# Halved block loads, regrouped stores and a load held back for the first store, in a DoRA projection on one core

## The chip, the cores and the metric

The kernel runs on one core of one Trainium2 chip. The metric is the device time of one execution in microseconds (us), as the median of several runs; lower is better. A core has five engines with an instruction stream each: TensorE (PE, its weight loads shown apart as PEld), VectorE (DVE), ScalarE (ACT), GpSimd (POOL) and SyncE (SP). They meet through semaphores. Transfers between HBM and the on-chip memory (SBUF) are issued by SP and by ACT here, each with a DMA queue of its own (q1 for SP, q10 for ACT), and are carried out by 16 DMA engines that serve both queues.

## What is computed

The reference, cut to what matters (x is 16 x 2048 x 256, W is 256 x 256, the LoRA rank is 16, all float32):

```python
W_adapted = W + scale * (lora_A @ lora_B)
W_norm = np.sqrt(np.sum(W_adapted ** 2, axis=0, keepdims=True) + 1e-8)
W_final = W_adapted / W_norm * m
y = x.reshape(-1, 256) @ W_final
```

So there is a small prologue that makes a 256 x 256 weight, and then one product over 32768 rows. x is 33.6 MB that are read, y is 33.6 MB that are written.

## The kernel before

**Tiling.** The rows are cut into 8 blocks of 4096 rows (4 MB each); a block is 8 chunks of 512 rows (512 KB), 64 chunks in all. Two chunks make a pair; there are 32 pairs. A block lies in one of five SBUF buffers (`x_bufs`, 128 partitions x 32 rows x 1 KB), so block 5 can be loaded only when block 0 has been stored from the same buffer. The product is written back over the x it came from. Inside a block each partition holds 32 consecutive rows, so a whole block is moved in pieces of 32 KB for each partition, half a block in pieces of 16 KB, and one chunk in pieces of 4 KB that lie 32 KB apart in HBM.

**One pair's way.** POOL rounds a pair to bf16 (L197, `xb`). TensorE transposes it in 8 steps into PSUM (`turned`, L302). DVE copies that to SBUF (L238, `xt`). TensorE multiplies, 8 matmuls for each of the two chunks (`product`, L316). ACT copies each chunk's product from PSUM over the chunk in `x_bufs` (L256). On TensorE the order is: turned(pair 0), and then a loop in which turned(p+1) stands ahead of product(p). TensorE takes one from the semaphores `rounded`, `copied` and `room` by hand (`take`).

**Prologue.** TensorE makes A^T and A·B (L272, L276), the column sums of squares (`n2_ps`, L283) and m spread over the partitions (`mb_ps`, L288), in that order. DVE makes `wa`, its square, `m_all` (L225), `wam` (L228), the reciprocal (L231) and `w_final` (L234); ACT makes the square root (L248). POOL's first rounding waits for DVE's fourth result (L192). Ahead of its loop TensorE waits until `w_final` is there (`dv` 8) and opens `room`; in that wait stands everything behind turned(0), turned(1) included.

**Loads (SP, in order).** W; then chunks 0-1, 2-3, 4-7; then blocks 1, 2 and 3 whole; then five chunks of block 4 and its last three chunks one by one (pieces of 4 KB). All these are issued at once, by 6 us. Then SP waits (L167) for stores 0, 1 and 2 and issues blocks 5, 6 and half of 7; the last half waits for store 3.

**Stores (ACT, in order).** Each stands behind ACT's copy of a chunk and a drain (L262). Block 0 behind chunk 21, block 1 behind chunk 22, block 2 in two halves behind chunk 24 (stores 0 to 3). Then chunks 24, 25, 26 and 27 one by one in pieces of 4 KB behind chunk 27; the rest of block 3 and blocks 4 and 5 behind chunk 47; block 6 behind chunk 55; block 7 in two halves behind chunks 59 and 63.

**Rest.** POOL holds pair 15 back until store 2 has landed (`REST`). At the very end SP waits for the later stores (L341).

Of the kernel before, what the change touches and what calls it, by code (L numbers as in the profile page):

```python
# [11 lines left out]
def kernel(  # L12
# [10 lines left out]
    nc = tc.nc  # L23
# [6 lines left out]
    x_flat = x.flatten_outer_dims()  # L30
    out_flat = out.flatten_outer_dims()
# [4 lines left out]
    J = 4  # L36
    DJ = 32
    BLK = DJ * P
    NBLK = N // BLK
# [3 lines left out]
    XBUFS = 5  # L43
    CH = DJ // J
    NCH = NBLK * CH

    NPR = NCH // 2
# [1 line left out]
    NXB = 2  # L49

    REST = 15
    IDLE = 8
    NXT = 2
    F8 = 2 * J * P

# [7 lines left out]
    def sb(name, shape, dtype):  # L63
        return ctx.enter_context(nc.sbuf_tensor(name, shape, dtype))
# [4 lines left out]
    x_bufs = [sb(f"x_sb{k}", [P, DJ, IN], FP32) for k in range(XBUFS)]  # L69
    xb_bufs = [sb(f"xb{k}", [P, 2 * J, IN], BF16) for k in range(NXB)]  # L70
# [4 lines left out]
    m_row = sb("m_row", [1, OUT], FP32)  # L75
    identity = sb("identity", [P, P], FP32)
    zeros = sb("zeros", [P, P], FP32)
    ones = sb("ones", [P, P], FP32)
# [18 lines left out]
    mb_ps = y_ps[1][:, 2, :]  # L97
# [3 lines left out]

    units = [(b * CH, CH) for b in range(NBLK - 1)]
    units += [(NCH - CH, CH // 2), (NCH - CH // 2, CH // 2)]
    loads = [(0, 2), (2, 2), (4, CH - 4)] + units[1 : XBUFS - 1]


    loads += [((XBUFS - 1) * CH, CH - 3)]
    loads += [(XBUFS * CH - 3 + c, 1) for c in range(3)] + units[XBUFS:]
    load_of = {g: n for n, (g0, cnt) in enumerate(loads) for g in range(g0, g0 + cnt)}

    F = NBLK - XBUFS
    G = F * CH
    stores = [(b * CH, CH, 21 + b) for b in range(F - 1)]
    stores += [(G - CH, CH // 2, 24), (G - CH // 2, CH // 2, 24)]
    FIRST = len(stores)
    stores += [(G + c, 1, G + 3) for c in range(4)]
    stores += [(G + 4, CH - 4, 47)]  # L120
    stores += [(b * CH, CH, max(47, (b + 1) * CH - 1)) for b in range(F + 1, NBLK - 1)]
    stores += [(g0, cnt, g0 + cnt - 1) for g0, cnt in units[-2:]]
    HALF = FIRST - 2


    late = [nc.alloc_semaphore(f"store{n}") for n in range(FIRST, len(stores))]
    sems = {f"store{FIRST + k}": s for k, s in enumerate(late)}

    def sem(name):
        if name not in sems:  # L130
            sems[name] = tc.alloc_semaphore(name)
        return sems[name]

    def in_sbuf(g0, cnt):
        b, c = divmod(g0, CH)
        return x_bufs[b % XBUFS][:, c * J : (c + cnt) * J, :]

    def in_dram(dram, g0, cnt):
        (u0, ucnt), = [u for u in units if u[0] <= g0 < u[0] + u[1]]
        unit = dram[u0 * J * P : (u0 + ucnt) * J * P].rearrange("(p j) k -> p j k", p=P)  # L140
        return unit[:, (g0 - u0) * J : (g0 - u0 + cnt) * J, :]

    def load_x(n):
        nc.sync.dma_start(
            out=in_sbuf(*loads[n]), in_=in_dram(x_flat, *loads[n])
        ).then_inc(sem(f"load{n}"), 16)

    def store_y(n):
        nc.scalar.dma_start(
            out=in_dram(out_flat, *stores[n][:2]), in_=in_sbuf(*stores[n][:2])  # L150
        ).then_inc(sem(f"store{n}"), 16)


    nc.sync.dma_start(
        out=w_nat[:], in_=W.rearrange("(p t) o -> p t o", t=KC)
    ).then_inc(sem("load_w"), 16)
    nc.scalar.dma_start(
        out=a_nat[:], in_=lora_A.rearrange("(p t) r -> p t r", t=KC)
# [1 line left out]
    nc.scalar.dma_start(out=b_nat[:], in_=lora_B).then_inc(sem("load_b"), 16)  # L160
    nc.scalar.dma_start(out=m_row[:], in_=m[None, :]).then_inc(sem("load_m"), 16)
    for n in range(len(loads)):
        if loads[n][0] == XBUFS * CH:


            for k in range(HALF + 1):
                nc.sync.wait_ge(sem(f"store{k}"), 16)  # L167
        if loads[n] == units[-1]:
            nc.sync.wait_ge(sem(f"store{HALF + 1}"), 16)
        load_x(n)  # L170


# [3 lines left out]
        out=identity[:],  # L176
        in_=zeros[:],
# [3 lines left out]
        pattern=[[-1, P]],  # L181
        channel_multiplier=1,
    ).then_inc(sem("ident"), 1)
    for p in range(NPR):
        b, c = divmod(p, PRB)
        for g in (2 * p, 2 * p + 1):
            if g == 0 or load_of[g - 1] != load_of[g]:
                nc.gpsimd.wait_ge(sem(f"load{load_of[g]}"), 16)
        if p == 0:


            nc.gpsimd.wait_ge(sem("dve"), 4)  # L192
        if p == REST:
            nc.gpsimd.wait_ge(sem(f"store{HALF}"), 16)
        if p >= NXB:
            nc.gpsimd.wait_ge(sem("turned"), p - NXB + 1)
        nc.gpsimd.tensor_copy(  # L197
            out=xb_bufs[p % NXB][:],
            in_=x_bufs[b % XBUFS][:, 2 * c * J : 2 * (c + 1) * J, :],
        ).then_inc(sem("rounded"), 1)  # L200

    nc.gpsimd.wait_ge(sem("turned"), NPR - NXB + 1)
    nc.gpsimd.memset(xb_bufs[NPR % NXB][:], 0.0).then_inc(sem("rounded"), 1)  # L203


    for _ in range(IDLE):
        nc.gpsimd.wait_ge(sem("ident"), 1)


    dv = sem("dve")  # L210
    nc.vector.memset(ones[:], 1.0)
# [8 lines left out]
        out=wa[:], in0=ab_ps, scalar=float(scale), in1=w_nat[:], op0=ALU.mult, op1=ALU.add  # L220
    ).then_inc(dv, 1)
    nc.vector.wait_ge(dv, 3)
    nc.vector.tensor_mul(out=sq[:], in0=wa[:], in1=wa[:]).then_inc(dv, 1)  # L223
    nc.vector.wait_ge(sem("pe"), 4)
    nc.vector.tensor_copy(out=m_all[:], in_=mb_ps).then_inc(dv, 1)  # L225
    nc.vector.wait_ge(dv, 5)
    for t in range(KC):
# [5 lines left out]
    for t in range(KC):  # L233
        i = nc.vector.tensor_mul(out=w_final[:, t], in0=wam[:, t], in1=rnorm[:])  # L234
    i.then_inc(dv, 1)
    for p in range(NPR):
        nc.vector.wait_ge(sem("turned"), p + 1)
        nc.vector.tensor_copy(  # L238
            out=xt_bufs[p % NXT][:].rearrange("p r t -> p (r t)").bitcast(FP32),
            in_=xt_ps[p % 2][:],  # L240
        ).then_inc(sem("copied"), 1)


    nc.scalar.wait_ge(dv, 1)

    nc.scalar.activation(out=warm[:], in_=eps_col[:], func=AF.Sqrt)  # L246
    nc.scalar.wait_ge(sem("pe"), 3)
    nc.scalar.activation(  # L248
        out=norm[:], in_=n2_ps, func=AF.Sqrt, bias=eps_col[:]
    ).then_inc(sem("act"), 1)  # L250
    drains = 0
    for g in range(NCH):
        b, c = divmod(g, CH)
        nc.scalar.wait_ge(sem("product"), g + 1)

        nc.scalar.copy(  # L256
            out=x_bufs[b % XBUFS][:, c * J : (c + 1) * J, :], in_=y_ps[g % 2][:]
        ).then_inc(sem("room"), 1)
        due = [n for n in range(len(stores)) if stores[n][2] == g]
        if due:  # L260
            drains += 1
            nc.scalar.drain().then_inc(sem("done"), 1)  # L262
            nc.scalar.wait_ge(sem("done"), drains)
            for n in due:
                store_y(n)


    pe = sem("pe")
# [6 lines left out]
    for t in range(KC):  # L275
        i = nc.tensor.matmul(  # L276
            ab_ps[:, t, :], aT[:, t * P : (t + 1) * P], b_bf[:], start=True, stop=True
        )
    i.then_inc(pe, 1)
    nc.tensor.wait_ge(dv, 4)  # L280

    for t in range(KC):
# [1 line left out]
            n2_ps, ones[:], sq[:, t, :], start=(t == 0), stop=(t == KC - 1)  # L284
        )
    i.then_inc(pe, 1)
    nc.tensor.wait_ge(sem("load_m"), 16)
    nc.tensor.matmul(mb_ps, ones[0:1, :], m_row[:], start=True, stop=True).then_inc(pe, 1)  # L288
    def take(name):

        nc.tensor.sem_inc(sem(name), -1).wait_op(sem(name), 1, "sem-ge")  # L291
# [4 lines left out]
        j_order.append(a + J // 2)  # L296

    def turned(p):
        take("rounded")

        for j in range(2 * J):
            i = nc.tensor.transpose(  # L302
                xt_ps[p % 2][:, j * P : (j + 1) * P],
                xb_bufs[p % NXB][:, j, :].bitcast(FP32),
                identity[:],
            )
        i.then_inc(sem("turned"), 1)

    def product(p):
        take("copied")  # L310
        for h in range(2):
            take("room")
            for t in range(KC):
                for j in j_order:
                    r = (h * J + j) * P
                    i = nc.tensor.matmul(  # L316
                        y_ps[h][:, j, :],
                        xt_bufs[p % NXT][:, r : r + P, t],
                        w_final[:, t, :],
                        start=(t == 0 and (j % (J // 2)) == 0),  # L320
                        stop=(t == KC - 1 and (j % (J // 2)) == (J // 2) - 1),
                    )
            i.then_inc(sem("product"), 1)

    turned(0)

    nc.tensor.wait_ge(dv, 8)
    nc.tensor.sem_inc(sem("room"), 2)
    with nc.Fori(0, NPR // 2, 1, engines=[PE], head_slot={PE: 128}):
        turned(1)  # L330
        product(0)
        turned(0)
        product(1)

# [1 line left out]
    critical.close()  # L336
    tc.close()
    tc.compile()
    for s in late:
        nc.sync.wait_ge(s, 16)  # L340
        nc.sync.sem_clear(s)  # L341


# [33 lines left out]
```

## Time and profile before

| what | value |
|---|---|
| median of 4 runs | 162.58 us (162.35 to 162.65) |
| the profiled execution's own time | 162.84 us |
| its span, first to last instruction | 161.5 us |
| moved by DMA | 67.42 MB, 417 GB/s over the span |
| busy: PE / PEld / DVE / ACT / POOL | 60% / 52% / 28% / 40% / 39% |
| TensorE idle in the middle (pair 15 held back) | 25 us, about 55 to 80 us |
| last product stored by ACT | issued at 132.25 us |

The profile's page has the span in 40 slices of 4.04 us with each engine's busy share, the DMA engines' busy share and the bytes that they moved; the chain of work that ended last; groups of instructions with their mean duration; and the DMA issues with the time from issue to landing. Besides the page, the timeline lists instructions in order of time, and the trace holds one record for each DMA packet (queue, start, duration, size) and the time of each semaphore update, a DMA's 16 completions among them. An engine that is idle costs something only where the last work of all waits for it.

### The profile page before, as it was taken

What the parts mean: (1) busy time and instruction counts of PE and PEld (TensorE: products, weight loads), DVE (VectorE), ACT (ScalarE), POOL (GpSimd) and SP (SyncE); (2) the same over time, 40 slices, a digit from 0 to 9 for tenths busy, and PEclk for the clock granted to TensorE, in tenths of its full rate; (3) what the DMA queues carried; (4) which work ended last, traced back from release to release, by engine and by line L of the source; (5) the groups of instructions that cost most, each with busy time, mean ns of one, the idle gap of its engine ahead of it and who ended that gap; (6) DMA issues with size and microseconds to landing.
All of it is one profiled execution on the core that took longest, in us unless ns stands there. A gap on an engine that the chain in (4) does not pass through costs nothing. (4 is left out here: it accounts for less than half of the span.)

```text
span 161.5 us, 2012 instructions
## 1 busy us (share of the span) xinstructions
PE 96.7 (60%) x786; PEld 84.8 (52%) x786; DVE 44.9 (28%) x44; ACT 64.0 (40%) x67; POOL 62.7 (39%) x39
## 2 busy tenths in 40 slices
PE   0493999999999600000199999999999940000000
PEld 0253798999998400000179999978899930000000
DVE  0447344354444300000033635353535300000000
ACT  3010366767767700000026686856786850000000
POOL 1264419677672000000674479197677100000000
PEclk9999999999999965555559999999999995555555
DMA  4999999999899999999999999999999999999895
GB/s 152 428 467 454 389 511 398 389 487 422 373 413 385 430 451 416 430 402 434 430 455 420 406 448 429 430 422 430 434 458 454 398 446 456 389 446 462 373 434 239
DMA packets 4356, 67.42 MB, mean 417 GB/s; under 512 B 625, under 2 KB 642, under 8 KB 1666
## 3 DMA queue, kind: packets, MB, share of 16 engines
q1 hardware_dynamic: 2160, 33.82, 49.4%
q10 hardware_dynamic: 2194, 33.59, 48.6%
q14 instruction: 2, 0.02, 0.0%
HBM read 33.85 MB, written 33.55 MB: 417 GB/s over the span
## 5 line engine op out<-in xcount | busy, mean ns | idle before, releaser
L256 ACT COPY x_sb<-y_ps 128x1024 f32<-128x1024 f32 x64 | 62.1, 1015 | 60.5 <-PE y_ps L316 59.9
L197 POOL CAST xb<-x_sb 128x2048 bf16<-128x2048 f32 x32 | 60.2, 1896 | 61.5 <-DMA out_dram<-x_sb 28.6
L316 PE MATMUL y_ps<-w_final,xt 128*128 128x256 bf16 x512 | 64.8, 282 | 0.8 <-PEq L291 0.7
L238 DVE COPY xt<-xt_ps 128x1024 f32<-128x1024 f32 x32 | 39.2, 1225 | 74.9 <-PE xt_ps L302 74.9
L316 PEld LDWEIGHTS y_ps<-w_final,xt 128*128 128x128 bf16 x512 | 51.6, 101 | 8.5 <-issue 1.5
L302 PE MATMUL xt_ps<-identity,xb 128*128 128x128 f32 x264 | 37.4, 288 | 27.8 <-PEq L291 27.6
L302 PEld LDWEIGHTS xt_ps<-identity,xb 128*128 128x128 f32 x264 | 32.3, 150 | 30.0 <-issue 29.6
L283 PE MATMUL y_ps<-sq,ones 128*128 128x256 f32 x4 | 2.1, 674 | 1.6 <-DVE sq L223 1.6
L272 PE MATMUL y_ps<-identity,a_nat 128*16 128x128 f32 x2 | 0.6, 394 | 3.7 <-DMA a_nat<-in_lora_A_dram 3.7
L248 ACT ACTIVATE norm<-y_ps,eps_col 128x256 f32<-128x256 f32 x1 | 0.5, 474 | 5.2 <-PE y_ps L283 5.2
L283 PEld LDWEIGHTS y_ps<-sq,ones 128*128 128x128 f32 x4 | 1.2, 323 | 2.3 <-DVE sq L223 2.1
L246 ACT ACT_TABLE_LOAD x1 | 1.3, 1283 | 2.4 <-issue 2.4
L203 POOL MEMSET xb<- 128x2048 bf16 x1 | 1.8, 1806 | 0.7 <-PE xt_ps L302 0.7
L272 PEld LDWEIGHTS y_ps<-identity,a_nat 128*16 128x16 f32 x2 | 0.1, 90 | 3.6 <-issue 3.6
L231 DVE RECIPROCAL rnorm<-norm 128x256 f32<-128x256 f32 x1 | 1.7, 1740 | 0.0
L225 DVE COPY m_all<-y_ps 128x256 f32<-128x256 f32 x1 | 0.4, 425 | 3.3 <-PE y_ps L288 3.3
L288 PE MATMUL y_ps<-m_row,ones 1*128 1x256 f32 x2 | 1.2, 710 | 0.0
L214 DVE CAST b_bf<-b_nat 16x256 bf16<-16x256 f32 x1 | 0.3, 281 | 2.9 <-DMA b_nat<-in_lora_B_dram 2.9
L219 DVE SCALAR_TENSOR_TENSOR wa<-y_ps,w_nat 128x512 f32<-128x512 f32 x1 | 0.7, 692 | 0.8 <-PE y_ps L276 0.8
L276 PE MATMUL y_ps<-b_bf,aT 16*128 16x256 bf16 x2 | 0.6, 402 | 0.5 <-DVE aT L216 0.5
L288 PEld LDWEIGHTS y_ps<-m_row,ones 1*128 1x128 f32 x2 | 0.5, 308 | 0.7 <-issue 0.7
L228 DVE TENSOR_TENSOR wam<-wa,m_all 128x256 f32<-128x256 f32 x2 | 0.8, 438 | 0.0
(13 smaller groups left out, 3.3 us busy)
## 6 DMA issues: line engine op xcount, KB each, us to landing
x_sb<-in_x_dram SPq DMA_DIRECT2D x5, 4096.0 KB, 26.1
out_dram<-x_sb ACTq DMA_DIRECT2D x5, 4096.0 KB, 23.6
out_dram<-x_sb ACTq DMA_DIRECT2D x5, 2048.0 KB, 29.2
x_sb<-in_x_dram SPq DMA_DIRECT2D x3, 2048.0 KB, 31.6
x_sb<-in_x_dram SPq DMA_DIRECT2D x1, 2560.0 KB, 44.8
x_sb<-in_x_dram SPq DMA_DIRECT2D x2, 1024.0 KB, 6.1
out_dram<-x_sb ACTq DMA_DIRECT2D x4, 512.0 KB, 51.9
x_sb<-in_x_dram SPq DMA_DIRECT2D x3, 512.0 KB, 47.4
```

The costliest lines, as they stand in the source:

```text
L197: nc.gpsimd.tensor_copy(out=xb_bufs[p % NXB][:], in_=x_bufs[b % XBUFS][:, 2 * c * J : 2 * (c + 1) * J, :],).then_inc(sem("rounded"), 1)
L203: nc.gpsimd.memset(xb_bufs[NPR % NXB][:], 0.0).then_inc(sem("rounded"), 1)
L219: nc.vector.scalar_tensor_tensor(out=wa[:], in0=ab_ps, scalar=float(scale), in1=w_nat[:], op0=ALU.mult, op1=ALU.add).then_inc(dv, 1)
L228: i = nc.vector.tensor_mul(out=wam[:, t], in0=wa[:, t], in1=m_all[:])
L231: nc.vector.reciprocal(out=rnorm[:], in_=norm[:]).then_inc(dv, 1)
L238: nc.vector.tensor_copy(out=xt_bufs[p % NXT][:].rearrange("p r t -> p (r t)").bitcast(FP32), in_=xt_ps[p % 2][:],).then_inc(sem("copied"), 1)
L246: nc.scalar.activation(out=warm[:], in_=eps_col[:], func=AF.Sqrt)
L256: nc.scalar.copy(out=x_bufs[b % XBUFS][:, c * J : (c + 1) * J, :], in_=y_ps[g % 2][:]).then_inc(sem("room"), 1)
L283: i = nc.tensor.matmul(n2_ps, ones[:], sq[:, t, :], start=(t == 0), stop=(t == KC - 1))
L288: nc.tensor.matmul(mb_ps, ones[0:1, :], m_row[:], start=True, stop=True).then_inc(pe, 1)
L302: i = nc.tensor.transpose(xt_ps[p % 2][:, j * P : (j + 1) * P], xb_bufs[p % NXB][:, j, :].bitcast(FP32), identity[:],)
L316: i = nc.tensor.matmul(y_ps[h][:, j, :], xt_bufs[p % NXT][:, r : r + P, t], w_final[:, t, :], start=(t == 0 and (j % (J // 2)) == 0), stop ...
```

## The change

- **First stores.** Block 0 is stored behind chunk 23 (not 21), block 1 behind chunk 24 (not 22), the two halves of block 2 behind chunk 25 (not 24).
- **Held loads.** The last three chunks of block 4 (three loads with pieces of 4 KB) wait on SP until store 0 has landed. They are now one entry in three pieces that count on one semaphore. Blocks 5 and on stand behind them in SP's order and wait for stores 0 to 2 as before.
- **Half loads.** Blocks 1, 2 and 3 are loaded in two halves each (pieces of 16 KB instead of 32 KB), so POOL can start on a block when its first half is there.
- **First pair.** ACT instead of POOL rounds pair 0, as soon as load 0 is there; POOL starts with pair 1, which waits for DVE's sixth result, and pair 2 waits for the eighth.
- **Prologue's order.** TensorE makes `mb_ps` ahead of `n2_ps`; the wait for `w_final` and the opening of `room` move from TensorE to DVE, so turned(1) no longer stands behind them.
- **Fill.** Waits that are always met, 8 behind POOL's work and 24 behind DVE's (before: 8 on POOL).
- The four 4 KB stores of chunks 24 to 27 are written as one entry in four pieces with one semaphore; their sizes, order and place stay.

The core of the diff:

```diff
-    loads = [(0, 2), (2, 2), (4, CH - 4)] + units[1 : XBUFS - 1]
-    loads += [((XBUFS - 1) * CH, CH - 3)]
-    loads += [(XBUFS * CH - 3 + c, 1) for c in range(3)] + units[XBUFS:]
+    H = XBUFS * CH
+    loads = [(0, 2, 2 * J), (2, 2, 2 * J)] + [(g0, 4, 4 * J) for g0 in range(4, 32, 4)]
+    loads += [(H - CH, 5, 5 * J), (H - 3, 3, J)]
+    loads += [(b * CH, CH, CH * J) for b in range(XBUFS, NBLK - 1)]
+    loads += [(g0, cnt, cnt * J) for g0, cnt in units[-2:]]
-    stores = [(b * CH, CH, 21 + b) for b in range(F - 1)]
-    stores += [(G - CH, CH // 2, 24), (G - CH // 2, CH // 2, 24)]
+    stores = [(0, CH, CH * J, 23), (CH, CH, CH * J, 24)]
+    stores += [(G - CH, 4, 4 * J, 25), (G - 4, 4, 4 * J, 25)]
-    stores += [(G + c, 1, G + 3) for c in range(4)]
-    stores += [(G + 4, CH - 4, 47)]
+    stores += [(G, 4, J, G + 3), (G + 4, CH - 4, (CH - 4) * J, 47)]
...
     for n in range(len(loads)):
-        if loads[n][0] == XBUFS * CH:
-            for k in range(HALF + 1):
-                nc.sync.wait_ge(sem(f"store{k}"), 16)
-        if loads[n] == units[-1]:
-            nc.sync.wait_ge(sem(f"store{HALF + 1}"), 16)
+        if loads[n][0] == H - 3:
+            wait_store(nc.sync, 0)
+        if loads[n][0] == H:
+            for k in range(FIRST - 1):
+                wait_store(nc.sync, k)
+        if loads[n] == loads[-1]:
+            wait_store(nc.sync, FIRST - 1)
         load_x(n)
...
-    for p in range(NPR):
+    for p in range(1, NPR):
...
-        if p == 0:
-            nc.gpsimd.wait_ge(sem("dve"), 4)
+        if p == 1:
+            nc.gpsimd.wait_ge(sem("dve"), 6)
+        if p == 2:
+            nc.gpsimd.wait_ge(sem("dve"), 8)
...
-    nc.vector.wait_ge(sem("pe"), 4)
+    nc.vector.wait_ge(sem("pe"), 3)
...
+    nc.vector.wait_ge(dv, 8)
+    nc.vector.sem_inc(sem("room"), 2)
...
+    for engine, idle in ((nc.gpsimd, 8), (nc.vector, 24)):
+        for _ in range(idle):
+            engine.wait_ge(sem("ident"), 1)
...
-    nc.scalar.wait_ge(sem("pe"), 3)
+    wait_load(nc.scalar, 0)
+    nc.scalar.copy(out=xb_bufs[0][:], in_=x_bufs[0][:, 0 : 2 * J, :]).then_inc(
+        sem("early"), 1
+    )
+    nc.scalar.wait_ge(sem("pe"), 4)
...
+    nc.tensor.wait_ge(sem("load_m"), 16)
+    nc.tensor.matmul(mb_ps, ones[0:1, :], m_row[:], start=True, stop=True).then_inc(pe, 1)
     nc.tensor.wait_ge(dv, 4)
...
-    nc.tensor.wait_ge(sem("load_m"), 16)
-    nc.tensor.matmul(mb_ps, ones[0:1, :], m_row[:], start=True, stop=True).then_inc(pe, 1)
...
+    nc.tensor.wait_ge(sem("early"), 1)
     turned(0)
-
-    nc.tensor.wait_ge(dv, 8)
-    nc.tensor.sem_inc(sem("room"), 2)
     with nc.Fori(0, NPR // 2, 1, engines=[PE], head_slot={PE: 128}):
+        take("rounded")
         turned(1)
         product(0)
+        take("rounded")
         turned(0)
         product(1)
```

## The prediction

> **What bounds the kernel now.** I read the page first: its rows for DMA.
>
> ```profile
> span 161.5 us, 2012 instructions
> ...
> DMA  4999999999899999999999999999999999999895
> GB/s 152 428 467 454 389 511 398 389 487 422 373 413 385 430 451 416 430 402 434 430 455 420 406 448 429 430 422 430 434 458 454 398 446 456 389 446 462 373 434 239
> ```
>
> The DMA engines are full from the second slice to the last but one, while no compute engine passes 60%. Then the chain of work that ended last, and what SP waited for:
>
> ```profile
> 130.22 1.01 ACT x_sb L256
> 131.23 0.91 ACTq L262
> ```
>
> ```profile
> SPq L341 <- DMA out_dram<-x_sb: 26.9, 4, 9.7
> ```
>
> All computing is over at 132.2; the other 29 us are stores. So the span is bytes over rate plus every stretch in which the DMA engines are empty or slow. Compute counts only where it leaves a queue without work. I asked the DMA view for stretches; an undisturbed one (118 to 150) gives 432 GB/s. One stands out, 48.9 to 52.1:
>
> ```profile
> DMA packets 266, 0.97 MB, mean 302 GB/s; under 512 B 30, under 2 KB 30, under 8 KB 266
> q1 hardware_dynamic: 266, 0.97, 99.2%
> ```
>
> Here the engines are busy and yet slow. These are the 4 KB pieces of block 4's last three chunks, alone on q1. In the packet records such a piece takes 159 ns undisturbed, here up to 724. The same records give 1213 ns for 32 KB, 611 for 16 KB, 309 for 8 KB. The timeline tells why nothing else fills the stretch:
>
> ```profile
> 47.96 0.37 ACTq L149 DMA_DIRECT2D out_dram<-x_sb  x1
> 48.55 1.01 ACT L256 COPY x_sb<-y_ps 128x1024 f32<-128x1024 f32 x1 [0.69 <-PE y_ps L316]
> ```
>
> Store 0 is issued at 47.96, but its first packet starts at 52.17. From then on the 4 KB loads lie beside stores and take 159 ns each, at 432 GB/s in total.
>
> **The change, part by part.**
>
> *Held 4 KB loads: -0.85 us.* Undisturbed pieces run at 16 x 4096 B / 159 ns = 412 GB/s. The slow stretch loses 3.2 us x (1 - 302/412) = 0.85; the packet records agree (384 pieces take 4.63 us of 16 engines' time, undisturbed 3.82). After the change these loads start some 3.5 us behind store 0's end, beside store 1 and the two halves of block 2. Before, from 52.6 on, 4 KB loads beside 32 KB stores cost 159 ns, so I take their excess as gone. From below: it stays whole, 0. Capacity fits: one 4 KB piece passes for each store piece, each engine has about 4 store pieces of block 1 left by then, 16 of block 2, and 24 pieces to load; the last few go beside the 4 KB stores, which need 32 and find the 32 pieces of blocks 5 to 7. No queue runs dry.
>
> *Half loads: +0.24 us.* Two pieces of 16 KB take 1222 ns against 1213; per engine and block 16 x 611 - 8 x 1213 = 72 ns, three blocks 0.22, with three more completion packets of 9 ns 0.24. By landings likewise: a 2 MB load took 4.90 us (8.90 to 13.80), a 4 MB load 9.72. This is on the path: the DMA engines have no slack to hide it. q1 without the held loads thus runs dry at 48.58 (end of its last 20 KB piece) + 0.24 = 48.8.
>
> *The hand-over from loads to stores* is the new cost: now nothing lies in q1 behind 48.8, so store 0 must be ready. When does chunk 23 come? Start-up rows of the timeline:
>
> ```profile
> 10.09 1.97 PE L302 MATMUL xt_ps<-identity,xb 128*128 128x128 f32 x8
> ...
> 13.15 0.76 DVE L234 TENSOR_TENSOR w_final<-wam,rnorm 128x256 bf16<-128x256 f32 x2
> ...
> 14.57 1.94 PE L302 MATMUL xt_ps<-identity,xb 128*128 128x128 f32 x8 [2.51 <-PEq L291]
> ...
> 16.30 3.62 PE L316 MATMUL y_ps<-w_final,xt 128*128 128x256 bf16 x16
> ...
> 20.94 1.91 PE L316 MATMUL y_ps<-w_final,xt 128*128 128x256 bf16 x16
> ...
> 23.57 3.74 POOL L197 CAST xb<-x_sb 128x2048 bf16<-128x2048 f32 x2 [5.09 <-DMA x_sb<-in_x_dram]
> ```
>
> TensorE waited 2.51 us for `w_final` with pair 1 rounded since 10.85. After: m lands at 6.41, `mb_ps` 6.45 to 7.6 (its 1.15 us from 8.94), the sums of squares to 9.6, square root to 10.2, reciprocal 1.74 and `w_final` 0.76 to 12.75 (before 13.9). ACT's rounding of pair 0 runs from 6.6, when load 0 lands; its length is not in the trace: between 1.0 (a 1024-element copy from PSUM) and 2.0 (two of them), I take 2.0, to 8.6, a microsecond ahead of TensorE and of the square root on the same engine. turned(0) and turned(1) end by 13.5, the first `xt` copy (1.22) by 14.05, and product(0) starts at 14.05 instead of 16.30: -2.25. POOL's wait of 5.09 us for block 1 goes too (its half lands at 18.8, before 23.5), and with it 0.34 us of TensorE's idle time.
>
> The clock adds to this. Product(0) took 3.6 us and product(1) 1.9: matmuls went from 421 to 272 ns at 20.4, after 5.8 us of unbroken work (at 85.2 after 5.0). After the change TensorE has work from 6.45 to 13.5, so product(0) most likely runs fast: another -1.7. Pairs then follow every 2.62 us (20.94, 23.56). Before, chunks 22 and 23 would have left ACT at 50.5 without the store between them (two copies, 1.93 from 48.55). After: 47.9 with a slow product(0), 46.2 with a fast one. Store 0 is issued 0.1 later, while q1 still has 0.7 to 2.5 us of work.
>
> From issue to first packet the trace has both ends: 1.03 us (`a_nat`) and 1.36 (W) on idle engines; 4.21 (store 0) and 3.52 (block 5, 78.23 to 81.75) beside a full queue. At 81.75 the newcomer came just as the last piece of the store ahead (81.71) had started: it waits for what the engines have taken in. In the new kernel that work ends at 48.8, so with issue at 46.3 I take a gap of **0**; with 48.0 it is 0.3 to 0.6; if the long delay were fixed, 1.7 to 3.4.
>
> The Trainium skill gives a price too: "DMA: Bandwidth & Descriptors", section Specifications, has about 0.6 us to the first byte for SP and ACT. By that even the late issue would have no gap and the sum would be -0.61 in both cases; the rows above are longer, and the sum goes by them.
>
> *Late stores and REST: 0.* Store 2 lands at about 75.7 instead of 78.13 (48.8, 16 pieces of 1.213, 8 of 0.611, some 12 of 0.159, and 0.7 to the last landing as before), pair 15 starts earlier, and block 5, behind the 4 KB loads in q1, still lands at about 93.2 (93.65). Cover: the stores behind chunk 47 are issued at 110.8, yet q10 has 4 KB pieces until 117.0; 6 us may be lost there for nothing. Stores 1 to 3 queue behind store 0 on q10 and lose nothing. *Fill waits* stand behind all work of their engines: 0. They and the new code may move instruction fetches; the trace has two packets of 8 KB, 0.31 us each, and one engine ends 0.84 us behind the next. A fetch more or less is +-0.3.
>
> **Sum.** -0.85 + 0.24 + 0 = -0.61 us. The profiled execution, 162.84, becomes 162.2 (span 160.9). The median of the runs shown lies 0.26 lower (162.58), and the same sum gives **162.0 us**.
>
> **The rivals.**
>
> 1. *Cold hand-over.* TensorE stays slow through product(0), or the early stage comes 1 to 2 us later than summed: issue at 48.0, gap 0.3 to 0.6, sum -0.3 to 0: 162.3 to 162.6, I say 162.4. For it: the speed-up came at different lengths of work (5.0, 5.8), and 5.1 us from 6.94 did not suffice.
> 2. *The long delay is fixed (slower).* A first store takes 3.5 to 4.2 us from issue whatever lies in q1. Place: 48.8 to store 0's first packet. Break-even is a gap of 0.61, first packet at 49.4, or 3.1 us from an issue at 46.3. Price at 46.3: gap 1.0 to 1.7, sum +0.4 to +1.1, 163.0 to 163.7; from 48.0 up to 165.4. For it: both delays in mid-kernel are that long. Against: both had other work in front.
> 3. *The 4 KB loads stay slow* beside stores for some other reason; then only the half loads count: 162.8. Against: 52.6 to 60. [...]
> 4. *More than summed:* a fetch less on the last engine, or less skew between engines: 161.5.
>
> **How the numbers follow.** Forecast 0.62 (own range 161.7 to 162.25), rival 1 0.14, rival 2 0.15, rival 3 0.05, rival 4 0.04. Range 161.5 to 163.1: it takes in 1, 3, 4 and the near end of 2 and leaves out the rest of 2. About 0.2% (0.33 us) is what a measurement tells from no change; faster is below 162.25, slower above 162.9. Faster: forecast 0.59, 4, and 0.05 of rival 1, 0.68. Same: 0.03 of the forecast, 0.06 of rival 1, 0.03 of rival 3, 0.12. Slower: rival 2, the rest of 1 and 3, 0.20.
>
> **What would show it.** Right: 4 KB packets near 159 ns throughout and the DMA view at 430 GB/s in every stretch from 4 to 159 us; store 0 issued at 46 to 48, its first packet within 0.3 us of q1's last; product(0) at 14 with 272 ns matmuls; landings of blocks 1 to 3 some 0.08 us later each. Wrong: q1 and q10 both empty for over 0.6 us around 49, or 4 KB packets of several hundred ns around 63 to 82, or an engine that ends far behind the others at the last store.

## The result and the profile after

The changed kernel takes 162.69 us (median of 33 runs, 162.38 to 164.54), the kernel before 162.5 us beside it (54 runs, 162.25 to 162.92): ratio 1.0033, with a 95% interval from 1.0021 to 1.0045. So it is a little slower, where 0.6 us less was forecast. The runs of the changed kernel fall in two groups: 19 from 162.38 to 162.79 (median 162.60), and 14 from 163.23 to 164.54 (median 163.64); expectations below that speak of 13 miscount by one. The 54 runs of before have no second group. Two things have to be explained: why the lower group is no faster than before, and where the upper group comes from.

The profiled execution took 162.55 us and is of the lower group. From its page, span, busy share of the DMA engines, and rate in the 40 slices:

```profile
span 161.2 us, 2026 instructions
...
DMA  4999999999999999999999999999999999999995
GB/s 157 429 455 415 439 423 423 447 406 447 439 406 504 406 390 441 409 438 424 427 423 432 430 455 423 417 441 423 403 480 423 398 476 415 406 480 415 394 439 232
```

The thirteenth slice (48.4 to 52.4), where before had 373 GB/s, has 504; the span is 0.3 us shorter. The start and store 0, from the timeline:

```profile
6.57 1.90 ACT L263 CAST xb<-x_sb 128x2048 bf16<-128x2048 f32 x1 [2.70 <-DMA x_sb<-in_x_dram]
...
9.43 3.38 PE L320 MATMUL xt_ps<-identity,xb 128*128 128x128 f32 x16
...
11.96 0.76 DVE L240 TENSOR_TENSOR w_final<-wam,rnorm 128x256 bf16<-128x256 f32 x2
...
14.39 1.91 PE L334 MATMUL y_ps<-w_final,xt 128*128 128x256 bf16 x16 [1.58 <-PEq L310]
...
46.32 0.37 ACTq L145 DMA_DIRECT2D out_dram<-x_sb  x1
```

Product(0) starts at 14.39 (forecast 14.05) and is fast, and store 0 is issued at 46.32 (forecast 46.3). In the packet records its first packet is at 48.47, while q1's last 20 KB pieces still run; the held 4 KB loads take 159 to 167 ns from 63 to 82. The end of the chain and SP's last wait are those of before:

```profile
130.33 1.01 ACT x_sb L275
131.34 0.92 ACTq L281
```

```profile
SPq L359 <- DMA out_dram<-x_sb: 27.0, 4, 9.7
```

A loss that before's first profile does not have stands later. The DMA view from 113.5 to 115.5, where the 4 KB stores have run out (their last piece ends at 113.55; in before's first profile at 116.69) and 16 KB loads lie alone in q1:

```profile
DMA packets 58, 0.79 MB, mean 393 GB/s; under 512 B 10, under 2 KB 10, under 8 KB 10
```

Seventeen of these loads take up to 1042 ns instead of 611. Below, such a loss is given as *excess*: the sum of all packets' time over their undisturbed time, shared among 16 engines. Here it is 0.27 us; before's 4 KB loads had 0.8. (Run 5 will show that another execution of before has this later loss too.) And one engine ends last: the 16 engines end at 159.7 on average and one at 160.7 (before 160.0 and 161.0). In the packet records of both kernels one engine carries its 32 KB stores in some 1265 to 1315 ns instead of 1213 while computing runs beside pure stores, about 120 to 135. It loses some 0.7 to 0.9 us there, as far as packets can be put to engines from their times, and mostly it is the one that ends last and sets the span.

### The profile page after: what moved, and what is told of

It is laid out like the page before. It is cut to its first block, busy times and chain, and to the rows that moved or that the text cites. A ratio compares the mean times of both kernels' runs of the same rounds, so it can differ in the third digit from the quotient of the medians.

```text
span 161.2 us, 2026 instructions
## 1 busy us (share of the span) xinstructions
PE 93.0 (58%) x786; PEld 83.1 (52%) x786; DVE 45.0 (28%) x44; ACT 65.6 (41%) x68; POOL 60.8 (38%) x38
## 5 line engine op out<-in xcount | busy, mean ns | idle before, releaser
L207 POOL CAST xb<-x_sb 128x2048 bf16<-128x2048 f32 x31 | 58.3, 1896 | 63.6 <-DMA out_dram<-x_sb 30.4
L334 PE MATMUL y_ps<-w_final,xt 128*128 128x256 bf16 x512 | 61.9, 274 | 2.0 <-PEq L310 1.9
L334 PEld LDWEIGHTS y_ps<-w_final,xt 128*128 128x128 bf16 x512 | 50.2, 99 | 8.4 <-issue 2.6
L320 PE MATMUL xt_ps<-identity,xb 128*128 128x128 f32 x264 | 36.5, 285 | 30.9 <-PEq L310 30.9
L263 ACT CAST xb<-x_sb 128x2048 bf16<-128x2048 f32 x1 | 1.9, 1898 | 2.7 <-DMA x_sb<-in_x_dram 2.7
L240 DVE TENSOR_TENSOR w_final<-wam,rnorm 128x256 bf16<-128x256 f32 x2 | 0.8, 422 | 0.0
```

Of the source, the lines that this page charges most:

```text
L207: nc.gpsimd.tensor_copy(out=xb_bufs[p % NXB][:], in_=x_bufs[b % XBUFS][:, 2 * c * J : 2 * (c + 1) * J, :],).then_inc(sem("rounded"), 1)
L263: nc.scalar.copy(out=xb_bufs[0][:], in_=x_bufs[0][:, 0 : 2 * J, :]).then_inc(sem("early"), 1)
L320: i = nc.tensor.transpose(xt_ps[p % 2][:, j * P : (j + 1) * P], xb_bufs[p % NXB][:, j, :].bitcast(FP32), identity[:],)
L334: i = nc.tensor.matmul(y_ps[h][:, j, :], xt_bufs[p % NXT][:, r : r + P, t], w_final[:, t, :], start=(t == 0 and (j % (J // 2)) == 0), stop ...
```

## The experiments

Eighteen runs. "Before" is always the kernel before, run beside the variant on the same chip. A kernel is called by the number of its run.

**1 and 2. Block 0 stored one chunk earlier or later**, in the changed kernel:

```diff
-    stores = [(0, CH, CH * J, 23), (CH, CH, CH * J, 24)]
+    stores = [(0, CH, CH * J, 22), (CH, CH, CH * J, 24)]    # 1
+    stores = [(0, CH, CH * J, 24), (CH, CH, CH * J, 24)]    # 2
```

> Block 0 is stored behind chunk 22 instead of 23, all else as in the changed kernel, whose runs fall in two groups, 20 from 162.4 to 162.8 us and 13 from 163.2 to 164.5. Theory A, the hand-over: in the second group TensorE starts product(0) slow, store 0 is issued at 48.0 instead of 46.3, and the DMA engines are empty between the last early load and store 0. Then one chunk earlier (0.9 us and more) takes most of the gap away: the second group goes or comes below 163.2, the first stays at 162.5 to 162.6. Theory B, lone loads: the second group comes from the last 16 KB loads, which in the profile lie alone from 113.5 to 115.5 at 340 to 410 GB/s; then the groups and their shares stay as they are.

> Block 0 is stored behind chunk 24, 1.7 us later than in the changed kernel (48.0, and 49.7 where product(0) is slow), the early loads end at 48.9 as before. Theory A: nearly all runs now have a gap, of 0.4 to 0.8 us where product(0) is fast and of 2 to 2.5 where it is slow: 163.2 and more, up to 165, the lower group gone. Theory B: no change, or up to 0.5 us, since the end of the loads does not move.

Earlier: 162.62 (162.36 to 163.62, 12 runs; two above 163, where the changed kernel had 14 of 33), ratio 1.0011 [0.9995, 1.0027]. Store 0 is issued at 45.17, and lone 20 KB loads become slow, from 46.9 to 48.4, excess 0.63 us. So neither the 4 KB pieces nor their place in HBM are needed for slow loads. Later: 165.34 (6 runs: two at 163.7, four from 165.15 to 165.65), ratio 1.016 [1.0127, 1.0193]. In its profile (163.69) store 0 is issued at 47.99, its first packet is at 48.88, the engines stand empty for up to 0.48 us (0.3 on average), and then transfers are slow three times more: near 62 (excess 0.15), near 66 (0.2), and at 80, where block 5's loads come (0.44). Together that is 1.1 us. That profile's time is the upper group's, with an issue that the prediction had named for a slow product(0): 48.0.

**3. TensorE kept busy.** Seven transposes into unused PSUM behind turned(0); they change no result.

```diff
     turned(0)
+    for _ in range(7):
+        nc.tensor.transpose(y_ps[0][:, 0, 0:P], identity[:], identity[:])
```

> The changed kernel with seven more transposes of the identity on TensorE behind turned(0), into a PSUM bank that is not yet in use, so that TensorE has no pause of 1.6 us ahead of product(0). Theory A, with the clock as the cause of the two groups: TensorE is fast at product(0) in every run, the second group goes, median 162.5 to 162.6. If the groups stay, the clock at product(0) is not what parts them. Theory B: the groups stay.

162.56 (162.40 to 162.94, 11 runs), ratio 1.0009 [1.0000, 1.0018]: the upper group is gone, and what is left equals before. TensorE's pause ahead of product(0) was not shorter (1.68 us); the work ahead of it was denser.

**4. One more chunk of small stores**, so that no load lies alone near 114: chunk 28 too is stored in 4 KB pieces.

```diff
-    stores += [(G, 4, J, G + 3), (G + 4, CH - 4, (CH - 4) * J, 47)]
+    stores += [(G, 4, J, G + 3), (G + 4, 1, J, G + 4), (G + 5, CH - 5, (CH - 5) * J, 47)]
```

> The changed kernel with chunk 28 as well stored in pieces of 4 KB, behind chunk 28, so that q10 has 40 small pieces for each engine beside the 32 pieces of blocks 5 to 7 and does not run out of them. Theory B: no stretch under 425 GB/s from 112 to 118, about 0.3 us less in the profile, the second group goes, median about 162.3. Theory A: the stretch goes, the second group stays.

162.97 (162.76 to 164.49, 8 runs, 3 above 163.6), ratio 1.0051 [1.0025, 1.0078]. The stretch is clean (one slow packet), and yet the upper group stays. The lone loads near 114 are not its cause. Sparing them gained nothing either: the five lower runs, 162.76 to 162.98, lie above the changed kernel's.

**5 and 6. Before again, and before with its last three loads as one** (pieces of 12 KB):

```diff
-    loads += [(XBUFS * CH - 3 + c, 1) for c in range(3)] + units[XBUFS:]
+    loads += [(XBUFS * CH - 3, 3)] + units[XBUFS:]
```

> The kernel before, unchanged, for a second profile: the first one's execution took 162.84 us, 0.3 above the median of its runs (162.5), at a mean granted clock of 0.827, while most runs of it show 0.84. Theory C: in most runs TensorE is fast at product(0) already, store 0 is issued near 46.3 instead of 47.96, and the 4 KB loads lie alone for 1 to 2 us instead of 3.2, so a common run loses only 0.3 to 0.5 us on them and not 0.85; time 162.4 to 162.6, clock near 0.84. Theory D: the loss of 0.8 to 0.9 us is there in any run, and the changed kernel loses it again elsewhere; then 4 KB packets take 0.8 us of 16 engines' time too long here too.

> The kernel before with the last three chunks of block 4 as one load with pieces of 12 KB, nothing held. If small pieces alone on q1 cost 0.85 us in a common run (theory D): -0.8 to -1.0 us, 161.6. Theory C: -0.3 to -0.5, 162.0 to 162.2. If it isn't the size of the pieces but lone loads at the end of q1 that are slow: no gain.

The second profile of before (162.77) differs from the first. TensorE's product(0) started at 18.74 instead of 16.30, store 0 was issued at 49.67 instead of 47.96, and the same lone 4 KB loads were undisturbed; the DMA view from 48.9 to 52.1, where the first profile had 302 GB/s:

```profile
DMA packets 352, 1.31 MB, mean 408 GB/s; under 512 B 33, under 2 KB 33, under 8 KB 352
```

So the 0.85 is not in every run of before, which had been taken for granted. And this execution lost time elsewhere: 0.11 us at 80 to 83, and 0.29 near 114, where the first had next to nothing. Its DMA view from 113.5 to 115.5:

```profile
DMA packets 72, 0.76 MB, mean 379 GB/s; under 512 B 10, under 2 KB 10, under 8 KB 31
```

It was no faster for what it was spared near 50. With 12 KB pieces: 162.54 (11 runs), ratio 0.9999 [0.9989, 1.0008]; store 0 at 47.94 and lone 12 KB loads slow from 49.6 to 52.4, excess 1.0 us. The size of the pieces is not the cause.

**7 and 8. Kernel 3 without the hold**, with three 4 KB loads (7) and with one 12 KB load (8):

```diff
-        if loads[n][0] == H - 3:
-            wait_store(nc.sync, 0)
...
-    loads += [(H - CH, 5, 5 * J), (H - 3, 3, J)]    # 8 alone
+    loads += [(H - CH, 5, 5 * J), (H - 3, 3, 3 * J)]
```

> The kernel with TensorE kept busy (162.56 us, one group of runs) with the 4 KB loads issued at once, not held for store 0. Store 0 is issued at 46.2, so the 4 KB loads lie alone only until its first packet, some 1 to 2 us. Theory C: holding them is worth 0.3 to 0.5 us here, so 162.9 to 163.1. Theory D: 163.3 to 163.5. If lone loads cost nothing once store 0 comes early: 162.5 and no difference.

> The kernel with TensorE kept busy, block 4's last three chunks as one load with pieces of 12 KB, issued at once. There are no lone 4 KB loads, and 24 pieces of 4 KB for each engine (7 ns each over the rate of large ones, 0.18 us) become 8 of 12 KB: both theories expect 162.3 to 162.5, unless the loads' last pieces are slow when they are alone, whatever their size: then 162.6 to 163.0.

162.81 (12 runs), ratio 1.0026 [1.0013, 1.0038], and 162.9 (11 runs), 1.0021 [1.0011, 1.0032]. The lone loads are slow in both (excess 0.4 and 0.6). Against kernel 3's 1.0009 the hold is worth 0.0012 to 0.0017 of 162.5, which is 0.2 to 0.3 us, and the intervals overlap; even from the lower end of kernel 3's to the upper end of 7's it is 0.0038, or 0.62 us, still under the 0.85. Four of kernel 7's twelve runs lie above 163 (163.09 to 163.57), though TensorE was kept busy.

**9. The changed kernel again.**

> The changed kernel once more, for a second profile. Theory of the cold start (the group of runs near 163.65 has a slow product(0), TensorE having stood still for 1.6 us ahead of it): the chance of such a run is 13 in 33. If it comes, product(0) takes 3.5 us instead of 1.91, store 0 is issued near 48.0, and both queues are empty for 0.5 to 1 us around 49. Rival theory (the group comes from the stores): a run above 163.2 has a fast product(0), store 0 at 46.3, and slow packets elsewhere. If the run is below 162.8, it tells nothing of this, and only whether the lone loads near 114 are slow again.

162.62; product(0) fast, no slow load anywhere, and the last engine still ends at 160.8 (mean 159.5). The stores behind chunk 47 were issued at 113.31, not 110.92, and the 16 KB loads near 114 were undisturbed. It was no faster than the first (162.55), which lost 0.27 us there.

**10. Only the last chunk held back** (28 KB pieces for the rest):

```diff
-    loads += [(H - CH, 5, 5 * J), (H - 3, 3, J)]
+    loads += [(H - CH, 7, 7 * J), (H - 1, 1, J)]
...
-        if loads[n][0] == H - 3:
+        if loads[n][0] == H - 1:
```

> Seven chunks of block 4 in one load with pieces of 28 KB, only the last chunk held back. The first queue then runs dry at 51.3 instead of 48.9 (1 MB more at 430 GB/s). Theory of the lost cushion: a store 0 issued at 48.0 still finds work in front, so no run lies more than 0.6 above the median, which is 162.4 to 162.6. Rival theory (loads that lie alone between store 0's issue and its first packet are slow, whatever their pieces): 28 KB pieces alone from 47 to 51 are slow, 0.3 to 0.7 us, and the median is 162.7 to 163.0, without a second group.

162.71 (162.43 to 163.37, 11 runs; one above 163), ratio 1.0012 [1.0001, 1.0022]. As the rival had it, lone 28 KB loads are slow, from 47.7 to 50.9, excess 0.7 us; as the theory had it, the upper group is all but gone.

**11 and 12. One part of the change each.** 11 keeps the new start and the half loads, with before's stores (21, 22, 24) and nothing held. 12 is before with stores 23, 24, 25 and the hold.

```diff
-    stores = [(0, CH, CH * J, 23), (CH, CH, CH * J, 24)]    # 11, in the changed kernel
-    stores += [(G - CH, 4, 4 * J, 25), (G - 4, 4, 4 * J, 25)]
+    stores = [(0, CH, CH * J, 21), (CH, CH, CH * J, 22)]
+    stores += [(G - CH, 4, 4 * J, 24), (G - 4, 4, 4 * J, 24)]
...
-        if loads[n][0] == H - 3:
-            wait_store(nc.sync, 0)
...
-    stores = [(b * CH, CH, 21 + b) for b in range(F - 1)]    # 12, in the kernel before
-    stores += [(G - CH, CH // 2, 24), (G - CH // 2, CH // 2, 24)]
+    stores = [(b * CH, CH, 23 + b) for b in range(F - 1)]
+    stores += [(G - CH, CH // 2, 25), (G - CH // 2, CH // 2, 25)]
...
+        if loads[n][0] == XBUFS * CH - 3:
+            nc.sync.wait_ge(sem("store0"), 16)
```

> The changed kernel with the old stores (behind chunks 21, 22 and 24) and none of the loads held: what is left of the change is the start, the half loads and the fill. Store 0 is issued near 44 and lies beside the last loads. Theory of the lost cushion: no second group of runs, since a late product(0) only moves store 0 within work that is there anyway; median 162.5 to 162.8 (half loads +0.24, 4 KB loads slow or not as in the kernel before). Rival theory (the start itself makes the second group, in whatever order the transfers stand): some 4 runs in 10 lie 1 us above the rest.

> The kernel before with the stores behind chunks 23, 24 and 25 and its last three loads held for store 0; the start, the whole loads and the pool's order stay old. Store 0 is issued at 50.5 or a little later, while the first queue runs dry at 48.6. Theory of the lost cushion: the gap is 2.2 to 2.8 us, the slow 4 KB loads (0.85) are spared, and what the engines lose later when they come out of a gap in step is 1 to 1.5 us (as with block 0 behind chunk 24): 164.5 to 166. Rival theory (a first store takes 3.5 us and more from its issue, whatever is in front): the gap is 5 us, 167 or more.

11: 163.11 (162.79 to 163.47, 6 runs), ratio 1.0038 [1.0026, 1.0051]. Its profile (163.4) has, with the same code up to there, the slow product(0) that the prediction feared, as its timeline shows:

```profile
9.19 2.84 PE L318 MATMUL xt_ps<-identity,xb 128*128 128x128 f32 x16
...
14.15 3.51 PE L332 MATMUL y_ps<-w_final,xt 128*128 128x256 bf16 x16 [2.13 <-PEq L308]
```

The transposes became fast halfway (2.84 us for 16 instead of 3.38), so TensorE was done sooner, stood still for 2.13 us instead of 1.58, and product(0) took 3.51 us. With pauses of 0.97 to 1.90 us it took 1.91 in the seven other profiles of this start (the longest is kernel 2's, whose transposes also sped up on the way: 3.07 us). The Trainium skill ("TensorE: Matmul & The Clock Gate", section What's actually happening) has the clock decided in free-running windows of 3.4 us, so that the change falls where the window happens to lie; the rows fit that, and no run here isolates it.

12: 166.97 (166.22 to 168.05, 4 runs), ratio 1.0301 [1.0271, 1.0332], above what was expected. Store 0 is issued at 50.60. The DMA view from 49.1 to 51.4:

```profile
DMA packets 0, 0.00 MB, mean 0 GB/s; under 512 B 0, under 2 KB 0, under 8 KB 0
```

Both queues are empty for 2.9 us, from 48.61; the first packet comes at 51.48, 0.88 us after the issue. A fixed long delay, as rival 2 had it, is refuted. The rest is later excess as in 2: near 64, 70, 82 (0.4) and 116 (0.3).

**What the fourteen profiles so far have in common.** Set side by side, store 0's issue, its first packet and the loads that lie alone in q1:

| kernel | store 0 issued | its first packet | first slow load, after the issue | excess, us |
|---|---|---|---|---|
| before | 47.96 | +4.2 | +1.5 | 0.79 |
| 6, before, 12 KB | 47.94 | +4.6 | +1.7 | 1.00 |
| 1, behind 22 | 45.17 | +3.7 | +0.9 (most from +1.7) | 0.63 |
| 11, start only | 45.07 | +3.8 | +1.8 | 0.48 |
| 10, hold one | 46.20 | +4.2 | +1.5 | 0.72 |
| 7, 8, unheld | 46.47, 46.50 | +3.6, +4.0 | +2.5, +2.1 | 0.38, 0.62 |
| changed, 9, 3, 4 | 46.1 to 46.3 | +2.2 to +2.4 | none | 0 |
| 5, before again | 49.67 | +2.4 | none | 0 |
| 2, 12 (q1 dry before the first packet) | 47.99, 50.60 | +0.9 | none | 0 |

In kernels 1, 6, 7, 8, 10, 11 and before, the loads had 4 us and more to go when the first store was issued to the idle queue, and were slow until that store's first packet. In the others the loads ended within 2.8 us of the issue and were undisturbed. This gave a new theory: it is the issue to the idle queue, not chance and not the pieces.

**13 to 15. Only the issue moved**, with the loads not held. 13: before with blocks 0 and 1 behind chunks 22 and 23. 14: behind 23 and 24, block 2 behind 25. 15: kernel 8 with block 0 behind chunk 26, blocks 1 and 2 behind 27.

```diff
-    stores = [(b * CH, CH, 21 + b) for b in range(F - 1)]
+    stores = [(b * CH, CH, 22 + b) for b in range(F - 1)]    # 13
+    stores = [(b * CH, CH, 23 + b) for b in range(F - 1)]    # 14
-    stores += [(G - CH, CH // 2, 24), (G - CH // 2, CH // 2, 24)]    # 14
+    stores += [(G - CH, CH // 2, 25), (G - CH // 2, CH // 2, 25)]
...
-    stores = [(0, CH, CH * J, 23), (CH, CH, CH * J, 24)]    # 15, in kernel 8
-    stores += [(G - CH, 4, 4 * J, 25), (G - 4, 4, 4 * J, 25)]
+    stores = [(0, CH, CH * J, 26), (CH, CH, CH * J, 27)]
+    stores += [(G - CH, 4, 4 * J, 27), (G - 4, 4, 4 * J, 27)]
```

> The kernel before with block 0 stored behind chunk 22 and block 1 behind chunk 23 (one chunk later each), nothing else. Store 0 is issued at 49.6 instead of 47.96; the 4 KB loads end by 52.0. Theory of the issue (loads that lie alone in their queue become slow some 1.5 to 2.8 us after a store has been issued to the other queue, and stay so until its first packet; where they end within 2.5 us of the issue they are spared): the 4 KB loads take 159 ns each throughout, no gap, and the median is 162.0 to 162.3 if the runs of before lose the 0.8 of its profile, 162.4 if they seldom do. Rival theory (lone loads are slow by chance, whatever is issued beside them): slow 4 KB packets again, between 49 and 53, and the median stays within 0.1 of before.

> The kernel before with the stores behind chunks 23, 24 and 25 and nothing held: the kernel with the hold alone, without its hold. Store 0 is issued at 50.6, 1.5 us ahead of the end of the loads. Theory of the issue: no slow packet up to 52, no gap when chunk 23 comes in time, 0.5 to 1.5 us of gap when the start is a microsecond later: 162.0 to 162.4, some runs up to 163.5. Rival theory (chance): slow packets between 49 and 52 as in the kernel before, 162.5.

> The changed kernel with TensorE kept busy by seven transposes, the last three chunks of block 4 as one load that is not held (pieces of 12 KB, as in the run that gave 162.9 with slow packets at 48.5 to 50.8), and block 0 stored behind chunk 26, blocks 1 and 2 behind chunk 27. Store 0 is issued near 50.2 instead of 46.5; the loads end at 52. Theory of the issue: the 12 KB loads take 460 ns each, no gap, and the median is 0.4 to 0.6 below that run: 162.3 to 162.5, without a second group. Rival theory (chance): slow 12 KB loads near 50 as there, 162.8 to 163.0.

In all three profiles the loads are undisturbed, as expected against chance. The issue in 13, and its DMA view from 48.9 to 52.1 (302 GB/s before):

```profile
49.65 0.37 ACTq L149 DMA_DIRECT2D out_dram<-x_sb  x1
```

```profile
DMA packets 357, 1.43 MB, mean 447 GB/s; under 512 B 36, under 2 KB 36, under 8 KB 353
```

The same for kernel 8 and then kernel 15, from 48.5 to 50.8, with the same 12 KB loads:

```profile
DMA packets 74, 0.86 MB, mean 374 GB/s; under 512 B 14, under 2 KB 14, under 8 KB 14
```

```profile
DMA packets 91, 0.98 MB, mean 427 GB/s; under 512 B 11, under 2 KB 11, under 8 KB 11
```

The times do not follow: 162.32 (4 runs), ratio 0.9973 [0.996, 0.9985]; 162.59 (5 runs), 0.9998 [0.9984, 1.0012]; 163.17 (162.47 to 163.65, 6 runs), 1.0023 [1.0002, 1.0044]. What is spared near 50 is lost, in part in 13 and as a whole in 14 and 15, at the next two places where a queue takes over: at 80 to 83, where block 5's loads are issued (excess 0.2, 0.5, 0.55), and near 114 (0.16, 0.3, 0.4). Before's first profile has 0.0 at both, its second, spared near 50 like these, 0.11 and 0.29.

**16. The changed kernel a third time.**

> The changed kernel a third time, for one more profile of its two groups of runs. Theory of the cold start: if the run is above 163.2, product(0) takes 3.5 us, store 0 is issued near 48, and both queues are empty for about half a microsecond near 49; if it is below 162.8, product(0) takes 1.91. Rival theory (the upper group comes from the stores): product(0) takes 1.91 in either case. The theory of the issue adds: the lone loads near 114 are slow if the stores behind chunk 47 are issued by 111.5, and undisturbed if they are issued after 113.

162.37, product(0) fast; the lone loads near 114 slow again (0.29 us), with the stores behind chunk 47 issued at 110.68.

**17 and 18. Kernel 13 again, and kernel 13 with the stores behind chunk 47 moved behind chunk 50.**

```diff
-    stores += [(G + 4, CH - 4, 47)]
-    stores += [(b * CH, CH, max(47, (b + 1) * CH - 1)) for b in range(F + 1, NBLK - 1)]
+    stores += [(G + 4, CH - 4, 50)]
+    stores += [(b * CH, CH, max(50, (b + 1) * CH - 1)) for b in range(F + 1, NBLK - 1)]
```

> The kernel before with blocks 0 and 1 stored behind chunks 22 and 23, once more, beside a run that goes one step further. Theory of the issue: as the first time, 4 KB loads at 159 ns each, ratio to before 0.996 to 0.9985 (162.1 to 162.4 where before takes 162.5). Rival theory (the first result, of 4 runs, was the chip's or chance): ratio 0.999 to 1.001.

> The same, and the stores behind chunk 47 moved behind chunk 50. They are issued near 114.5 instead of 110.55, while the 16 KB loads that then lie alone end near 117.2. Theory of the issue, carried to the second place where it lost time (0.16 to 0.4 us of 16 engines between 113.5 and 116): no slow 16 KB load there, no gap at 117, and 0 to 0.2 below the run beside it, since one engine that is slow for another reason between 116 and 134 still ends last. Rival theory (chance): slow 16 KB loads as often as with the early issue. If the stores come too late for the first queue's end, a gap at 117 makes it slower by as much.

17: 163.55 (162.31 to 163.78, 6 runs), ratio 1.0061 [1.004, 1.0082]. The gain of 13 was a lucky draw: of the ten runs of this kernel five lie at 162.27 to 162.37, one at 162.94 and four at 163.48 to 163.78. It has a second group like the changed kernel's, with before's start (of the 17 runs of before beside it, two lie above 163: 163.02, 163.29). 18: 163.74 (162.5 to 164.25, 12 runs), ratio 1.0062 [1.0039, 1.0085]; its profile (163.9) shows an execution of the upper kind. Lines of its timeline:

```profile
4.95 0.28 DVE L214 CAST b_bf<-b_nat 16x256 bf16<-16x256 f32 x1 [3.73 <-DMA b_nat<-in_lora_B_dram]
...
13.94 1.90 POOL L197 CAST xb<-x_sb 128x2048 bf16<-128x2048 f32 x1 [2.31 <-DMA x_sb<-in_x_dram]
13.99 2.45 DVE L234 TENSOR_TENSOR w_final<-wam,rnorm 128x256 bf16<-128x256 f32 x2
...
18.83 3.55 PE L316 MATMUL y_ps<-w_final,xt 128*128 128x256 bf16 x16
...
51.49 0.37 ACTq L149 DMA_DIRECT2D out_dram<-x_sb  x1
```

Here `lora_B` landed late: DVE rounds it at 4.95, in kernel 13 at 3.94, and the prologue was behind by 0.85 us at `w_final`. So POOL's rounding of pair 2, which waited for its load alone, started just ahead of `w_final` (13.99; in 13 at 13.14), which then took 2.45 us instead of 0.76. (The Trainium skill, "SBUF — State Buffer", section Who interferes with whom, has DVE and GpSimd share a port pair as an exclusive lock; the 1.69 us more beside a 1.90 us cast agree.) Product(0) came 2.5 us later than in 13 (18.83 against 16.28), store 0 1.8 us later, at 51.49. Its first packet was at 52.36, with up to 0.3 us of idle time on the engines ahead of it, and all 16 then began within 0.16 us. Then the price, in the DMA view from 80 to 83, when block 5's loads are issued:

```profile
DMA packets 98, 0.88 MB, mean 294 GB/s; under 512 B 15, under 2 KB 15, under 8 KB 58
```

That is an excess of 1.0 us; kernel 13 had 0.2 there. The late start in 5 has the same two causes (`lora_B` rounded at 4.86, `w_final` 2.45 us), but there store 0 stood behind chunk 21, and the unheld loads covered for it. The stores behind chunk 50 were issued at 116.05, later than summed: the lone loads were undisturbed (0.02 us), but the stores' own 16 KB pieces were slow from 117 on (up to 1390 ns instead of 611, excess 0.26 us). The second place is thus not settled by this run.

## Why the prediction was wrong

The range (161.5 to 163.1) held the median, but faster, with 0.68, was wrong. By its steps:

- **Held 4 KB loads, -0.85.** This step failed, and it is a term that was mis-sized. The mechanism holds: held, the pieces take 159 ns. But the 0.85 is the loss of one execution of before. A second one, of nearly the same time, lost 0.08 there, and 0.4 at 80 and 114 instead; kernels 13 to 15, whose loads were undisturbed near 50 without a hold, lost time at the same two places. A loss at one take-over was counted as if nothing could come in its place at the next. The prediction took the profile's excess from the profile's time, and then took the same sum from the median, though its own table had that execution 0.26 above the median; both profiled executions of before (162.84, 162.77) lie among the slowest tenth of its 54 runs. Measured, the hold is worth 0.2 to 0.3 us (kernel 3 against 7 and 8), about what the half loads cost; so the lower group lies about where before lies.
- **Half loads, +0.24.** Right: q1's last 20 KB load lands at 49.30 instead of 49.07.
- **Hand-over, 0.** Met in all three profiles of the changed kernel: first packet at 48.36 to 48.49, q1 dry near 48.9. The issue at 46.3 is partly luck, as product(0) started 0.34 us later than summed. Most likely not met in the upper group: kernel 2, issued at 48.0, takes the upper group's time (163.69), kernel 11's slow product(0) makes all behind it 1.6 us later, kernel 3 with denser work has no such group. No execution of the changed kernel from that group was profiled, so for this kernel itself the slow product(0) is inferred. The sum had priced a late issue at 0.3 to 0.6, and the gap in kernel 2 is of that size (0.3); but the issue costs 1.1 (163.69 less the lower group's 162.60), since slow packets follow at 62, 66 and 80. That price stood nowhere. Rival 1 (cold hand-over) named the place and rival 2 (a gap makes it slower) the sign; its reason, a fixed delay of 3.5 to 4.2 us, is wrong.
- **The cover that went.** In before the loads that were not held lasted to 52.4, 3.8 us beyond 48.6, and hid a late store 0: execution 5 was 1.7 us late and lost nothing near 50. The prediction said that nothing lies in q1 behind 48.8, but summed the usual execution only, and not how far the start varies. That this made two groups where there had been one is argued from these runs.
- **Late stores, REST, 0.** Right in size: store 2 lands at 75.74 (forecast 75.7), block 5 at 93.8 (93.2). But the 16 KB loads near 114 lost 0.27 to 0.29 us in two profiles of three, where the text said that 6 us could be lost there for nothing. It had read from before that q10 has 4 KB pieces until 117; in the changed kernel they end at 113.5. No effect on the time is shown: the third profile, without this loss, took 162.62, the other two 162.55 and 162.37.
- **Fill and fetches, +-0.3.** Three fetch packets of 8 KB behind the start, where before had two, 0.31 us each: within what was allowed for.
- **What sets the end.** The sum moved all engines alike. Over three profiles of the changed kernel they end at 159.6 on average against 160.0 in before's first, but 159.6 in its second; the last, slow one ends at 160.5 to 160.8 against 161.0.
- Rival 3 is refuted (the pieces are not slow beside stores); rival 4 did not come.

Open stays why a DMA that is issued to an idle queue slows the other queue's packets until its own first packet, what slows one engine from 120 to 135, and why a loss that is spared at one take-over comes at the next. For upper runs a slow product(0) is not the only candidate: three of kernel 15's six are near 163.6 and four of kernel 7's twelve above 163 though TensorE was kept busy, and none of these was profiled. A late landing of `lora_B`, as in 5 and 18, is a rival that no run isolates; kernels 7 and 8 have it in their profiles too, and there `w_final` took its usual 0.76 us and store 0 came 0.3 us later than in kernel 3 (in the changed start POOL rounds pair 2 only behind `w_final`). No version here is surely faster than before; kernel 3 equals it.

## What to carry to other kernels

A loss read in one profiled execution is a term of that execution: profile the old kernel twice before you promise it for the median, and look where else the time goes in the execution that was spared. When you take work out of a queue because it seems wasted, ask what lateness it was hiding, and how late the next transfer is in the worst start, not in the usual one. A gap in full DMA queues cost more than its length in kernels 2 and 12.

## What was not expected of the hardware

- From issue to first packet a store took 0.9 us where the other queue had run dry by then on most engines (kernels 2, 12, 18), 1.5 to 2.4 us where the other queue was just ending (kernels 14 and 15 at 1.5; the first packet came 0.1 to 0.3 us ahead of the loads' mean end on the 16 engines), and 3.6 to 4.6 us where the other queue went on; in the last case the other queue's packets of any size (4 to 28 KB) became slow from about 1.5 to 2.5 us after the issue, with an excess of 0.4 to 1.0 us. The mirror image, loads issued beside full stores near 80, cost 0 to 1.0 us.
- After a gap all engines begin together (first packets within 0.16 us, against 0.3 us and more otherwise), and at the next take-over 0.4 to 1.0 us were lost near 81 in kernels 2, 12 and 18. That the common step is the cause is not shown: kernels 14 and 15, without a gap, lost 0.5 to 0.6 us there too.
- `w_final` on DVE took 2.45 us instead of 0.76 when a GpSimd rounding began within 0.06 us of it (5 and 18). The two met because `lora_B` had landed 0.8 to 1.0 us late; together this put product(0) 2.4 to 2.5 us later.
